# Where a transformer step loads its residual tiles, its first weight and one block's normed rows

## The chip, the cores and the metric

One core of a Trainium2 chip runs the whole program. Its engines are TensorE (PE, matmuls; PEld is its weight load), VectorE (DVE), ScalarE (ACT), GpSimd (POOL) and SyncE (SP), whose queue issues the data transfers here. Each engine takes its instructions strictly in the order in which they are written into its queue, and waits for semaphores on the way. The metric is device time in microseconds for one execution.

## The reference, cut to what matters

One layer of a streaming encoder runs on a prompt of 2048 tokens and a sample of 32, with width 1024, all in float32:

```python
def rmsnorm(x, g, eps=EPS):
    xf = x.astype(jnp.float32)
    y = xf * lax.rsqrt(jnp.mean(xf * xf, axis=-1, keepdims=True) + eps)
    return (y * g.astype(jnp.float32)).astype(x.dtype)

def ffn_ple(h, p, g_mlp, w_up, w_down, w_ple_gate, w_ple_proj):
    c = rmsnorm(h, g_mlp)
    h = h + jnp.square(jax.nn.relu(c @ w_up)) @ w_down
    return h + jax.nn.sigmoid(h @ w_ple_gate) * (p @ w_ple_proj)

# per layer, for the prompt and for the sample:
qa, ka, va, qb, kb, vb = split_proj(rmsnorm(hp, g_attn[i]), w_in[i])
oa = diff_attn_prompt(qa, ka, va, t5_table, lam)
ob = band_attn_prompt(qb, kb, vb, band_table[i])
hp = hp + merge(oa, ob, subln_g[i], out_norm_b[i], w_out[i], lam_init)
hp = ffn_ple(hp, p_prompt[i], g_mlp[i], w_up[i], w_down[i], w_ple_gate[i], w_ple_proj[i])
```

`diff_attn_prompt` and `band_attn_prompt` are two kinds of attention. The change touches neither; it touches the start of the first projection, the MLP and the gate.

## The kernel before, in words

**Precision.** Every float32 operand is split into a high part (`hi`, rounded by ScalarE) and a low part (`lo`, the difference, by VectorE or by GpSimd in pieces of 256 columns). `split` (L232 to 241) does that: L235 is ScalarE's high part, L241 VectorE's low part, L230 and L220 GpSimd's. `mm3` (L257 to 269) then does three matmuls for one product: high by high, low by high, high by low.

**Blocks.** The tokens are cut in four blocks: 0 (512), 1 (512 and the 32 of the sample), 2 and 3 (512 each). `HALVES` is (0, 1) and (2, 3). Activations lie transposed, 128 channels to a tile.

**The front.** `run` loads two tiles of rows of x, the constants, the first unit of the value weights `w_v` (512 KB), and then the first 256 columns of x transposed (`xcols`, two transfers of 512 KB, channels 0 to 511 and 512 to 1023). Three more weight units and the next 256 tokens follow. `prep` takes the squares of the rows (L393), the reciprocal root (`rsqrt`, L275 to 282), spreads it over the partitions with a transpose on TensorE (L397, tile `rp`), scales x with it (L405, tile `xt`) and splits the result into `aH` and `aL`. `proj` makes the value products: for the columns c = 0 and c = 1 of `w_v`, two units each, it splits the weights (`wunit`, tiles `wh` and `wl`), where VectorE does the low parts as long as `spare` is set, as it is in this first call. For the first 256 tokens and c = 0, `mm3` is told `high`: all high by high products come first, then those with the weight's low part, then those with the activation's (L264).

**The MLP of blocks 0 and 1.** `cnorm` fills `cH` and `cL`, the split of the normed rows, tile by tile, eight tiles of 128 channels. For block 1, `cpre` has written the normed rows to the DRAM tensor `cB` while block 0 ran. When block 0's units have been written, `cnorm(1, ...)` loads each row tile into a `tmp` tile and splits it into the one `act` pair, which block 0 has just used. `tmp` has three buffers, and the MLP's own relu tiles (L980, L981) use the same ring. The same pool has the tags `sh` and `sl` (one buffer each) and `acc` (two) of the same size, which the norms use. `mlp_down` adds its products from PSUM into h (L1001); the PSUM pool of these products has two banks here.

**The MLP of blocks 2 and 3.** The two blocks together are computed with seven products in place of eight (a Strassen-like scheme). `uphase` (L1120 to 1194) makes the seven combinations of the activations and stores them in the DRAM tensor `uS`; the stores of the last group stand at the end, after which its tiles' memory is given back. `dphase` (L1196 to 1250) then takes the seven products in the order 3, 5, 7, 4, 2, 6, 1. Each has eight steps c, each step two halves k. For a half it splits the activation (`dx`, four buffers, from `ut`, loaded from `uS`) and the weight (`dw`, from `wd`, or from the combination `dv` of two `wd`), and does 12 matmuls into four PSUM banks (tile `dp`). At a product's end its four banks are added into the tiles of h (L1249): product 3 into block 3's tiles 0 to 7, product 5 into block 2's tiles 0 to 3 and block 3's 0 to 3.

**Where h comes from.** h of blocks 2 and 3 (16 tiles of 256 KB) lies in the DRAM tensor `hS`. Its place in SBUF, `hh`, is where the tiles of `uphase` were. `hstep` is called in product 3 at k = 0 of each step. In the steps 0 to 3 it loads two tiles for each of the two blocks. Ahead of each load stands a copy of one column of the step's `dx` into the tile, on GpSimd (L1698); the load overwrites it, and so it cannot start before that step's `dx` is there, and the `dx` buffer is not free before the copy has read it.

**The gates.** Between the steps of `dphase`, `run` advances `gates()`, the gate of blocks 0 and 1: it loads h of the block in one transfer of 2 MB, splits it (`hH`, `hL`; the low parts of even tiles on GpSimd, of odd ones on VectorE), and then multiplies by `w_ple_gate` (tile `gps`) and `w_ple_proj` (`pps`). The weights, `ut` and `pn` share a ring of four buffers.

**What sets the order.** The program text gives each instruction a priority, and a planner with a simulated clock (`schedule_with_timeline_sim=True`) writes the queues: at each point it takes what it holds to be ready. Buffers and memory that are used again carry semaphore waits. All transfers go through SP's one queue, in order.

Of the kernel before, what the change touches and what calls it, by code (L numbers as in the profile page):

```python
# [12 lines left out]
F32 = mybir.dt.float32  # L13
# [31 lines left out]
HALVES = [(0, 1), (2, 3)]  # L45
# [81 lines left out]
def drain(gen):  # L127
    for _ in gen:
        pass
# [67 lines left out]
class Kern:  # L197
# [175 lines left out]
        self.dma(x[:n], src)  # L373
        return x

    def xcols(self, b, c0, n, pp):
        xt = pp.tile([P, 8, 256], F32, tag="xt", bufs=self.nx, name="xt")
        for k in range(0, 8, 4):
            self.dma(xt[:, k : k + 4, :n], self.xT[:, k : k + 4, T0[b] + c0 : T0[b] + c0 + n])
        return xt  # L380

    def prep(self, b, acts, pp, mm, tag, xs=()):
# [34 lines left out]
    def proj(self, half, grp, acts, sg, mm, vs=range(2), gs=range(4), spare=None):  # L417
        nc, a = self.nc, self.a
# [7 lines left out]
        u = {}  # L426
        for c, b, c0, n in order:
            if c not in u:
                lo = "dve" if spare else "pool"
                u[c] = [  # L430
                    self.wunit(a["w_v"][grp, i, c], [4, 256], "act", lo, spare if (c, i) == (1, 1) else None)
                    for i in range(2)
                ]
            aH, aL = acts[b]
            t0 = 512 * b + c0 if c0 < 512 else SP
            ps = mm.tile([P, 512], F32, tag="mm", name="vps")
            self.mm3(
                ps[:n, :256],
                [
                    (aH[:, k, c0 : c0 + n], aL[:, k, c0 : c0 + n], u[c][k // 4][0][:, k % 4], u[c][k // 4][1][:, k % 4])  # L440
                    for k in range(8)
                ],
                high=bool(spare) and c0 < 256 and c == 0,
            )
            raw = (Rings((spare, "vraw", 4)) if spare else self.vr).tile([P, 256], F32, name="vraw")
            nc.scalar.activation(raw[:n], ps[:n, :256], AF.Copy)
            hl = sg.tile([P, hc, 2, dv], F32R, tag="vhl", bufs=3, name="vhl")
            r3 = raw.rearrange("p (h d) -> p h d", d=dv)
            self.split(hl[:n, :, 0], hl[:n, :, 1], r3[:n], "dve", "pool")
            row = t0 if t0 < SP else t0 + PAST  # L450
            self.dma(
                self.vS[grp][row : row + n, 512 * c : 512 * c + 512],
                hl[:n].rearrange("p a b d -> p (a b d)"),
            )
            if t0 >= SP:
                self.dma(vo_s[0:n, 256 * c : 256 * c + 256], raw[:n])
            elif grp == 0:
                self.dma(vo_p[t0 : t0 + n, 256 * c : 256 * c + 256], raw[:n])
            elif t0 >= SP - 512:
                self.dma(vo_p[t0 - SP + 512 : t0 - SP + 512 + n, 256 * c : 256 * c + 256], raw[:n])  # L460
            yield
# [734 lines left out]
    def dphase(self, h, pool, md, step):  # L1196
        nc = self.nc
        def wrow(q, c):
            i, j = int(q[0]) - 1, int(q[1]) - 1
            r = pool.tile([P, 2, 512], F32, tag="wd", bufs=6, name="wd")  # L1200
            self.dma(r.rearrange("p a b -> p (a b)"), self.a["w_down"][8 * j + c, i])
            return r

        def operands(m, sq, so, c):
            ws = [wrow(q, c) for q in sq]
            u = self.rawp.tile([P, 2, 512], F32, bufs=self.nraw, name="ut")
            self.dma(u, self.uS[:, m - 1, 2 * c : 2 * c + 2])
            for k in range(2):
                x = pool.tile([P, 2, 512], F32R, tag="dx", bufs=4, name="dx")
                self.tsplit(x, u[:, k], "dve")  # L1210
                v = ws[0][:, k]
                if len(ws) == 2:
                    v = pool.tile([P, 512], F32, tag="dv", bufs=4, name="dv")
                    nc.vector.tensor_tensor(v, ws[0][:, k], ws[1][:, k], op=so)
                w = self.wp.tile([P, 2, 512], F32R, tag="wc", bufs=self.wtags[2], name="dw")
                self.tsplit(w, v, "dve")
                yield w, x

        add, sub = ALU.add, ALU.subtract
        plan = [  # L1220
            (3, ("11",), add, (("12", add), ("22", add))),
            (5, ("11", "12"), add, (("11", sub), ("12", add))),
            (7, ("12", "22"), sub, (("11", add),)),
            (4, ("22",), add, (("11", add), ("21", add))),
            (2, ("21", "22"), add, (("21", add), ("22", sub))),
            (6, ("21", "11"), sub, (("22", add),)),
            (1, ("11", "22"), add, (("11", add), ("22", add))),
        ]
        for m, sq, so, outs in plan:
            ps = [md.tile([P, 512], F32, tag="mm", name="dp") for _ in range(4)]  # L1230
            for c in range(8):
                for k, (w, x) in enumerate(operands(m, sq, so, c)):
                    if m == 3 and k == 0:
                        step(c, x)
                    for d in range(4):
                        sl = slice(P * d, P * d + P)
                        self.mm3(
                            ps[d], [(w[:, 0, sl], w[:, 1, sl], x[:, 0], x[:, 1])],
                            start=c + k == 0, stop=c == 7 and k == 1,
                        )  # L1240
                if c < 7:
                    yield
            adds = [(d, q, op) for d in range(4) for q, op in outs]
            if m == 1:
                adds.sort(key=lambda x: x[1])
            for d, q, op in adds:
                i, t = int(q[0]) - 1, int(q[1]) - 1
                hv = h[2 + t][4 * i + d]
                nc.vector.tensor_tensor(hv, hv, ps[d], op=op)  # L1249
            yield  # L1250
# [231 lines left out]
    def run(self):  # L1482
        tc, nc, a = self.tc, self.nc, self.a
        with ExitStack() as top:
# [25 lines left out]
            with ExitStack() as x:  # L1510
                self.nx = 2
                pp = opened(x, "pp0", 3, side="right")
                spare = opened(x, "w4", 1, side="right")
                xs = [self.xrows(0, P * i, P, pp) for i in range(2)]
                self.consts(cp)
                self.pre = [self.wraw(a["w_v"][0, 0, 0], [4, 256])]
                xs.append(self.xcols(0, 0, 256, pp))
                self.pre += [self.wraw(a["w_v"][0, i, c], [4, 256]) for c, i in ((0, 1), (1, 0), (1, 1))]
                xs += [self.xrows(0, 256 + P * i, P, pp) for i in range(2)]
                xs.append(self.xcols(0, 256, 256, pp))  # L1520
                wk = opened(x, "setup", 1, side="right")
                p0 = self.prep(0, acts, pp, ps_t, "tp", xs)
                p1 = self.prep(1, acts, pp, ps_t, "tp")
                su = self.setup(cp, wk, sg)
                for _ in range(5):
                    next(p0)
                front = Rings((mm, "mm"), (ps_s, "s"))
                self.warm(ps_o)
                for i, _ in enumerate(self.proj((0,), 0, acts, sg, front, spare=spare)):
                    if i in (0, 1, 2):  # L1530
                        next(p0, None), next(p0, None)
                    if i in (9, 11, 13, 15):
                        next(su)
                    if i > 7:
                        next(p1, None), next(p1, None)
                drain(su)
                drain(p1)
                self.nx = 1
            ppx = ExitStack()
            pp = opened(ppx, "pp", 1)  # L1540
# [4 lines left out]
            with ExitStack() as x:  # L1545
                pool = opened(x, "a0", 1, side="right")
# [40 lines left out]
            actq = Sized(opened(sq_, "actq", 2), BLK, True)  # L1587
# [9 lines left out]
            wk = opened(sq_, "wk", 1)  # L1597
# [20 lines left out]
            def hmove(b, h, load, ds=range(8)):  # L1618
                for d in ds:
                    x, y = h[d][:, : BN[b]], self.hS[:, d, T0[b] : T0[b] + BN[b]]  # L1620
                    self.dma(*((x, y) if load else (y, x)))
                return h
# [20 lines left out]

            for b in HALVES[0]:
                if b == 1:
                    drain(self.cnorm(1, wk, actq, cn))
                h = [hq.tile([P, BLK], F32, tag="h", bufs=8, name="h") for _ in range(8)]
                hmove(b, h, True)
                dn = Turn(mm)
# [42 lines left out]
            h = {b: hh.tile([P, 8, 512], F32, tag="h", name="h") for b in HALVES[1]}  # L1692
            h = {b: [t[:, d] for d in range(8)] for b, t in h.items()}

            def hstep(c, x):
                for b in HALVES[1] if c < 4 else ():
                    for d in (2 * c, 2 * c + 1):
                        nc.gpsimd.tensor_copy(h[b][d][:, :1], x[:, 0, :1].bitcast(F32))  # L1698
                    hmove(b, h[b], True, range(2 * c, 2 * c + 2))

            fk = opened(top, "fk", 1)
            udx, gqx = ExitStack(), ExitStack()
# [90 lines left out]
```

## Time and profile before

| | |
|---|---|
| median of 3 runs | 2963.94 us (2962.72 to 2965.97) |
| profiled execution | 2962.09 us, of which span 2960.3 us |
| PE busy | 2898.4 us (98%), 17041 matmuls |
| VectorE, ScalarE, GpSimd busy | 1759.7, 1761.3, 1377.7 us |
| data moved | 584.57 MB, mean 197 GB/s |
| mean granted clock of TensorE | 0.993 |

A row of a group or of the order of time names an engine, a line, the operation, and output <- input by the program's tile names; "x8" is a count. In brackets stands how long the engine was idle just before and what ended that wait. A row of the waits reads: who waited for whom, total us, times, longest. A line number can be that of a helper, so tile names say more. Copies and splits of many tiles share a line.

### The profile page before, as it was taken

The numbers are of one execution on the slowest core, as the hardware profiler recorded it, in microseconds if no ns is written. First come the engines' busy times: TensorE is split into PE (matmuls) and PEld (weight loads), VectorE is DVE, ScalarE is ACT, GpSimd is POOL, SyncE is SP. The second block draws the span as 40 slices with busy tenths as digits, with TensorE's granted clock in tenths as the row PEclk, the third lists the DMA queues.
The fourth block names the chain that finished last, engine by engine and source line by source line (L and its number), as shares of the span: only waits on it lengthen the run. The fifth ranks groups of instructions, "written<-read, shape, count | busy, mean of one in ns | idle before, by whom it ended". The sixth has DMA issues, their size and how long they took to land.

```text
span 2960.3 us, 49308 instructions
## 1 busy us (share of the span) xinstructions
PE 2898.4 (98%) x17041; PEld 2556.4 (86%) x17041; DVE 1759.7 (59%) x3930; ACT 1761.3 (59%) x3741; POOL 1377.7 (47%) x1911
## 2 busy tenths in 40 slices
PE   8999999999999999999999999999999989999998
PEld 7898998898889888888899999889788868888886
DVE  6565855444465543665665564447666556767955
ACT  5576757766666665767776675444555445545554
POOL 4677665533345455655554454440855533133000
PEclk9999999999999999999999999999999999999999
DMA  9977578776677644444743433666444395756811
GB/s 352 329 255 235 188 245 268 253 232 198 227 251 229 205 158 155 164 156 151 233 145 120 150 111 114 190 206 204 158 150 145 140 347 186 271 194 200 270 60 57
DMA packets 301513, 584.57 MB, mean 197 GB/s; under 512 B 34864, under 2 KB 132272, under 8 KB 301264
## 3 DMA queue, kind: packets, MB, share of 16 engines
q1 hardware_dynamic: 301264, 581.43, 58.7%
q8 instruction: 135, 2.21, 0.3%
q14 instruction: 114, 0.93, 0.1%
HBM read 450.10 MB, written 131.22 MB: 196 GB/s over the span
## 4 chain that ended last, share of the span: by engine, by line
PE 87%; DMA 5%; DVE 4%; ACT 2%; issue 1%; POOL 1%; SPq 0%; ACTq 0%; DVEq 0%; POOLq 0%
PE s L607 4%; PE ups L269 4%; PE ups L268 4%; PE ups L267 4%; PE qps L267 4%; PE qps L268 4%; PE qps L269 4%; PE dps L267 4%; PE dps L269 4%; PE dps L268 4%; PE xps L269 3%; PE xps L268 3%; PE xps L267 3%; PE dp L267 3%; PE dp L269 3%; PE dp L268 3%
## 5 line engine op out<-in xcount | busy, mean ns | idle before, releaser
L230 POOL TENSOR_TENSOR wl<-wr,wh 128x256 fp32r<-128x256 f32 x936 | 699.0, 778 | 688.9 <-ACT wh L235 600.5
L235 ACT ACTIVATE wh<-wr 128x1024 fp32r<-128x1024 f32 x270 | 284.8, 1056 | 181.5 <-issue 28.7
L267 PE MATMUL dps<-uh,wh 128*128 128x272 f32 (+1 forms) x768 | 249.8, 326 | 5.0 <-DVE h L1001 4.4
L267 PE MATMUL ups<-cH,wh 128*128 128x272 f32 (+1 forms) x768 | 249.1, 325 | 2.0 <-ACT wh L235 1.9
L269 PE MATMUL ups<-cH,wl 128*128 128x272 f32 (+1 forms) x768 | 249.1, 325 | 0.9 <-DVE wl L241 0.9
L268 PE MATMUL ups<-cL,wh 128*128 128x272 f32 (+1 forms) x768 | 249.7, 325 | 0.0
L268 PE MATMUL dps<-ul,wh 128*128 128x272 f32 (+1 forms) x768 | 247.7, 323 | 0.0
L269 PE MATMUL dps<-uh,wl 128*128 128x272 f32 (+1 forms) x768 | 247.4, 323 | 0.0
L267 PE MATMUL qps<-aH,wh 128*128 128x512 f32 (+3 forms) x640 | 229.1, 358 | 2.7 <-ACT wh L235 2.2
L269 PE MATMUL qps<-aH,wl 128*128 128x512 f32 (+3 forms) x640 | 227.5, 356 | 0.0
L268 PE MATMUL qps<-aL,wh 128*128 128x512 f32 (+3 forms) x640 | 227.2, 355 | 0.0
L268 PE MATMUL dp<-dx,dw 128*128 128x512 f32 x448 | 178.0, 397 | 0.0
L267 PE MATMUL dp<-dx,dw 128*128 128x512 f32 x448 | 168.1, 399 | 9.2 <-ACT dx L235 9.1
L607 PE MATMUL s<-ka,q 128*128 128x512 f32 (+3 forms) x640 | 174.2, 369 | 1.3 <-DMA q<-qS 0.7
L269 PE MATMUL dp<-dx,dw 128*128 128x512 f32 x448 | 174.9, 397 | 0.0
L267 PEld LDWEIGHTS dps<-uh,wh 128*128 128x128 f32 x768 | 144.2, 188 | 17.7 <-DVE h L1001 6.1
L267 PEld LDWEIGHTS ups<-cH,wh 128*128 128x128 f32 x768 | 144.4, 188 | 14.9 <-ACT wh L235 2.3
L613 DVE TENSOR_REDUCE nm<-s 128x1 f32<-128x512 f32 (+1 forms) x192 | 121.7, 640 | 57.1 <-PE s L607 55.8
L269 PEld LDWEIGHTS ups<-cH,wl 128*128 128x128 f32 x768 | 144.2, 188 | 12.7 <-DVE wl L241 1.4
L268 PEld LDWEIGHTS ups<-cL,wh 128*128 128x128 f32 x768 | 144.5, 188 | 11.3
L269 PEld LDWEIGHTS dps<-uh,wl 128*128 128x128 f32 x768 | 144.2, 188 | 11.0
L268 PEld LDWEIGHTS dps<-ul,wh 128*128 128x128 f32 x768 | 144.4, 188 | 10.4
(278 smaller groups left out, 8897.1 us busy)
## 6 DMA issues: line engine op xcount, KB each, us to landing
wd<-w_down SPq DMA_DIRECT2D x96, 512.0 KB, 5.1
q<-qS SPq DMA_DIRECT2D x128, 256.0 KB, 4.5
v<-vSa SPq DMA_DIRECT2D x64, 512.0 KB, 3.8
wr<-w_up SPq DMA_DIRECT2D x64, 512.0 KB, 3.7
wr<-w_down SPq DMA_DIRECT2D x64, 512.0 KB, 3.7
wr<-w_qk SPq DMA_DIRECT2D x58, 512.0 KB, 5.0
ut<-uS SPq DMA_DIRECT2D x56, 512.0 KB, 4.1
kS<-qk SPq DMA_DIRECT2D x32, 512.0 KB, 5.1
```

Of the source, the lines that this page charges most:

```text
L230: nc.gpsimd.tensor_tensor(out[:, sl], a[:, sl], b[:, sl], op=op)
L235: nc.scalar.activation(hi, raw, AF.Copy)
L267: nc.tensor.matmul(ps, lh, rh, start=start and i == 0, stop=False)
L268: nc.tensor.matmul(ps, lh, rl, start=False, stop=False)
L269: nc.tensor.matmul(ps, ll, rh, start=False, stop=stop and i == n - 1)
L607: nc.tensor.matmul(s, q[:, m, hl, P * qi : P * qi + nr], kt[:, m, k0 - kb : k0 - kb + n], start=hl == 0, stop=hl == 1)
L613: nc.vector.tensor_reduce(nmx, s, axis=AX.X, op=ALU.max, negate=True)
```

## The change

Three things are edited. In `dphase` the hook `step` is called at k = 0 of every product with its number, and `hstep` now loads one tile per step: block 3's tile c in step c of product 3, block 2's tile c in step c of product 5; the one-column copy ahead of it is on VectorE. In the front, `xcols` may call a function between its two transfers, and the first unit of `w_v` is loaded there, behind the first half of x transposed and not ahead of both; the low parts of the two units of c = 0 move from VectorE to GpSimd. In the MLP, `cnorm` of block 1 takes its row tiles in turn from `tmp`, `sh`, `sl` and `acc` and not from `tmp` alone.

```diff
-    def xcols(self, b, c0, n, pp):
+    def xcols(self, b, c0, n, pp, between=None):
         xt = pp.tile([P, 8, 256], F32, tag="xt", bufs=self.nx, name="xt")
         for k in range(0, 8, 4):
             self.dma(xt[:, k : k + 4, :n], self.xT[:, k : k + 4, T0[b] + c0 : T0[b] + c0 + n])
+            if k == 0 and between:
+                between()
         return xt
...
             if c not in u:
-                lo = "dve" if spare else "pool"
+                lo = "dve" if spare and c else "pool"
...
                 for k, (w, x) in enumerate(operands(m, sq, so, c)):
-                    if m == 3 and k == 0:
-                        step(c, x)
+                    if k == 0:
+                        step(m, c, x)
...
-                self.pre = [self.wraw(a["w_v"][0, 0, 0], [4, 256])]
-                xs.append(self.xcols(0, 0, 256, pp))
+                xs.append(self.xcols(0, 0, 256, pp, lambda: self.pre.append(self.wraw(a["w_v"][0, 0, 0], [4, 256]))))
...
                 if b == 1:
-                    drain(self.cnorm(1, wk, actq, cn))
+                    idle = Rings(*[(wk, t, n) for t, n in (("tmp", 3), ("sh", 1), ("sl", 1), ("acc", 2))])
+                    drain(self.cnorm(1, idle, actq, cn))
...
-            def hstep(c, x):
-                for b in HALVES[1] if c < 4 else ():
-                    for d in (2 * c, 2 * c + 1):
-                        nc.gpsimd.tensor_copy(h[b][d][:, :1], x[:, 0, :1].bitcast(F32))
-                    hmove(b, h[b], True, range(2 * c, 2 * c + 2))
+            def hstep(m, c, x):
+                b = {3: 3, 5: 2}.get(m)
+                if b:
+                    nc.vector.tensor_copy(h[b][c][:, :1], x[:, 0, :1].bitcast(F32))
+                    hmove(b, h[b], True, (c,))
```

`Rings` (L152 to 161) hands out tiles from its rings in turn.

## The prediction

> **What bounds the kernel.** I read the page first, then who TensorE (PE) waited for over the whole span, then the busy time by stretch, and last the instructions in order of time at the three places that the diff touches.
>
> ```profile
> span 2960.3 us, 49308 instructions
> PE 2898.4 (98%) x17041; PEld 2556.4 (86%) x17041; DVE 1759.7 (59%) x3930; ACT 1761.3 (59%) x3741; POOL 1377.7 (47%) x1911
> PE dp L267 <- ACT dx L235: 9.1, 2, 8.4
> PE rp L397 <- DVE rsy L282: 6.0, 1, 6.0
> PE dps L267 <- DVE h L1001: 4.4, 5, 2.0
> PE gps L267 <- ACT wh L235: 3.5, 1, 3.5
> PE qps L267 <- ACT wh L235: 2.2, 1, 2.2
> 0.00:20.00 20.00, 10.49 (x53) 9.88 (x54) 10.77 (x22) 12.86 (x23) 0.93 (x7) 0.74 0.95 336
> 1400.00:1440.00 40.00, 37.61 (x190) 31.36 (x189) 29.22 (x58) 28.47 (x61) 16.44 (x21) 1.00 0.63 201
> 2370.00:2430.00 60.00, 47.73 (x196) 37.38 (x194) 33.77 (x48) 24.54 (x44) 14.36 (x26) 0.94 0.98 378
> ```
>
> TensorE is busy for 2898.4 of 2960.3 us, and no edit takes a matmul away. So the change can only win back part of 61.9 us in which TensorE stands, plus time that it runs at a lower granted clock. In the stretch rows (length, then busy PE, PEld, DVE, ACT, POOL, then clock, DMA share, GB/s) the three places hold 9.5, 2.4 and 12.3 us of it. The first and third are also places where the DMA engines are full (0.95 and 0.98).
>
> **The largest place: the start of the down projection.** These are the instructions in order of time (start, length), the landing times of two loads there, and three stretches of 4 us.
>
> ```profile
> 2393.96 0.69 DVE L241 TENSOR_TENSOR dx<-ut,dx 128x512 fp32r<-128x512 f32 x1 [0.96 <-ACT dx L235]
> 2399.95 0.32 SPq L211 DMA_DIRECT2D uS<-u  x1
> 2400.67 8.74 POOL L220 TENSOR_TENSOR hL<-h,hH 128x256 fp32r<-128x256 f32 x8 [32.48 <-ACT hH L235]
> 2407.62 2.34 DVE L1214 TENSOR_TENSOR dv<-wd 128x512 f32<-128x512 f32 x2
> 2409.36 4.36 POOL L1698 COPY h<-dx 128x1 f32<-128x1 f32 x16
> 2410.39 1.15 ACT L235 ACTIVATE dx<-ut 128x512 fp32r<-128x512 f32 x2 [6.16 <-POOL h L1698]
> 2410.88 11.27 SPq L211 DMA_DIRECT2D h<-hS  x16
> 2411.07 2.07 PE L267 MATMUL dp<-dx,dw 128*128 128x512 f32 x4 [8.40 <-ACT dx L235]
> 2423.20 0.52 SPq L211 DMA_DIRECT2D wr<-w_ple_gate  x1
> 2429.24 1.06 ACT L235 ACTIVATE wh<-wr 128x1024 fp32r<-128x1024 f32 x1 [0.64 <-DMA wr<-w_ple_gate]
> 2430.36 0.50 PE L267 MATMUL gps<-hH,wh 128*128 128x512 f32 x1 [3.51 <-ACT wh L235]
> uS<-u SPq DMA_DIRECT2D x2, 256.0 KB, 5.3
> h<-hS SPq DMA_DIRECT2D x16, 256.0 KB, 5.7
> 2412.00:2416.00 4.00, 4.00 (x14) 3.10 (x13) 2.85 (x5) 2.09 (x5) 1.71 (x4) 0.71 0.99 371
> 2416.00:2420.00 4.00, 4.00 (x19) 3.22 (x18) 0.69 (x1) 0.27 (x1) 0.00 (x0) 1.00 1.05 395
> 2432.00:2436.00 4.00, 4.00 (x13) 3.11 (x13) 4.00 (x4) 2.48 (x4) 4.00 (x5) 0.65 0.73 238
> ```
>
> The chain reads backwards. TensorE waits 8.40 us for a split dx tile. There are four dx buffers, and each even one must first be read by a one-column copy on POOL (L1698). POOL is strictly in order, and its copies stand behind eight low-part pieces of the gate's h, which end at 2409.4. Then SP issues all sixteen loads of h in one burst of 11.27 us, and the gate's weight, queued behind them, lands 6.0 us after 2423.20. That is the second stand of 3.51 us. After each stand the clock is down: 14 and 13 matmuls are counted in 4 us where a full stretch counts 19, one every 0.21 us, so the restarts cost 5 x 0.21 = 1.1 and 6 x 0.21 = 1.3 us. Together 9.1 (both waits for dx) + 3.5 + 2.4 = 15.0 us.
>
> Part by part:
>
> *Copies from POOL to VectorE.* The wait on the eight pieces (2400.67 to 2409.4) goes. What is late next is the memory: h lies where the up phase's tiles lay, and the last of these leaves by the store at 2399.95, which lands 5.3 us later, at 2405.25. The earliest copy is there; ScalarE needs 0.68 us from dx to the matmul (2410.39 to 2411.07), so TensorE resumes at 2406.1 and 5.0 us of the 8.4 are saved. If VectorE, which is in order too, takes the copy only before its dv pair at 2407.62, it resumes at 2408.5 (2.6 saved); behind that pair at 2410.8 (0.3 saved). I take **3.7**, between the two likelier places. The slow restart of 1.1 I leave in.
>
> The Trainium skill ("TensorE: Matmul & The Clock Gate", section "What's actually happening") has the clock fall after an idle window of about 3.4 us; by that rule a stand of 3.4 us or less may restart at full clock, and the sum would be up to 1.1 us better. The row at 2430.36 (3.51 us idle, then 13 matmuls in 4 us) is just on the other side of it, so the trace agrees and leaves it open.
>
> *The loads, one per step.* The sixteen copies need not come in four steps any more: h of block 3 takes the eight steps of the first product, block 2 the eight of the second. At most six of the sixteen loads stand ahead of the gate's weight instead of sixteen; at 11.27 / 16 = 0.70 us each it is issued ten loads, 7.0 us, sooner, at 2416.2, and lands at 2422.2. TensorE gets there at 2426.85 (2430.36 - 3.51) less 3.7, at 2423.1. So the stand goes with its slow restart: **3.5 + 1.3 = 4.8**; if the queue stays as full as it is, nothing.
>
> *What the copies cost.* The trace has no one-column copy on VectorE. Bounds: 0.15 us by the nearest one-column row (L298 below), 0.27 by POOL's 4.36 / 16; sixteen are 2.4 to 4.4 us, hidden because VectorE is 59% busy. Queued behind each are the splits of dw and dx, for which TensorE waits; that is the third rival. The loads must land before the sums of their product: a tile copied with dx of the last step lands 5.7 us after issue, and four dx buffers ahead of the last matmul are four times twelve matmuls at 0.21, 10 us. Covered; without that cover up to 5.7 us.
>
> **The front.** In order of time:
>
> ```profile
> 5.95 0.15 DVE L298 TENSOR_SCALAR columns<-columns 128x1 f32<-128x1 f32 x1 [4.61 <-DMA columns<-columns]
> 7.58 1.06 ACT L235 ACTIVATE wh<-wr 128x1024 fp32r<-128x1024 f32 x1 [0.23 <-DMA wr<-w_v]
> 8.54 0.19 ACT L278 ACTIVATE rsy<-rsy 128x2 f32<-128x2 f32 x1
> 8.67 1.23 DVE L241 TENSOR_TENSOR wl<-wr,wh 128x1024 fp32r<-128x1024 f32 x1 [2.56 <-ACT wh L235]
> 10.70 0.66 PE L397 MATMUL rp<-ident,rsy 128*128 128x128 f32 x2 [6.01 <-DVE rsy L282]
> 11.40 3.22 DVE L405 SCALAR_TENSOR_TENSOR xt<-xt,columns,rp 128x256 f32<-128x256 f32 x8 [0.84 <-PE rp L397]
> 11.83 1.06 ACT L235 ACTIVATE wh<-wr 128x1024 fp32r<-128x1024 f32 x1 [3.10 <-DMA wr<-w_v]
> 13.46 2.07 PE L264 MATMUL vps<-wh,aH 128*128 128x256 f32 x8 [2.10 <-ACT aH L235]
> 33.60 5.67 POOL L230 TENSOR_TENSOR wl<-wr,wh 128x256 fp32r<-128x256 f32 x8 [3.38 <-ACT wh L235]
> 40.66 3.48 DVE L405 SCALAR_TENSOR_TENSOR xt<-xt,columns,rb 128x256 f32<-128x256 f32 x4 [8.55 <-ACT wh L235]
> 46.80 0.50 PE L267 MATMUL qps<-aH,wh 128*128 128x512 f32 x1 [2.20 <-ACT wh L235]
> ```
>
> Today the first weight's high part (1.06) stands ahead of the Exp on ScalarE, and its low part (1.23) ahead of the norm's small ops on VectorE. With the weight a half of x later, the Exp goes first (1.1 sooner) and the low part goes to POOL (1.2 sooner): rp and the first product up to 2.3 us earlier, at 11.2 for 13.46. POOL needs 5.67 / 8 x 4 = 2.8 us for a low part where VectorE needs 1.23; both are wanted only behind the high products, and the second unit's high part cannot begin before its load at 11.83, so its low part ends near 15.7, about when VectorE's did.
>
> POOL's pieces now run beside xt. An xt beside POOL took 3.48 / 4 = 0.87 us at 40.66 (row vector in SBUF), and 3.22 / 8 = 0.40 at 11.40 (row vector in PSUM, POOL idle). At 0.87 the eight xt would end 3.8 us later than at 0.40, and the gain of the second four is gone.
>
> The Trainium skill ("SBUF — State Buffer", section "Who interferes with whom") has a VectorE op with two inputs in SBUF and a reading GpSimd op block each other, which speaks against this edit. Both rows agree with it. At the edited place the vector is in PSUM, so by that rule only the aL splits would slow down and the front's gain would stay whole.
>
> The gain must also pass 46.80, where TensorE waits for a weight that ScalarE takes behind block 1's x, itself not begun before 40.66 with DMA full. If that stays put, all 2.3 us end there, the wait becomes 4.5 and a slow restart (1.3) is new. Bounds: 2.3 saved to 1.3 lost; I take **0.6**, near the middle.
>
> **The block boundary.**
>
> ```profile
> 1422.91 1.33 ACT L235 ACTIVATE cH<-tmp 128x544 fp32r<-128x544 f32 x2 [1.59 <-DMA tmp<-cB]
> 1424.31 0.68 DVE L1001 TENSOR_TENSOR h<-h,dps 128x512 f32<-128x512 f32 x1
> 1425.04 0.50 PE L267 MATMUL dps<-uh,wh 128*128 128x512 f32 x1 [2.03 <-DVE h L1001]
> ```
>
> ScalarE waits for a cB load that had no free tmp buffer, VectorE behind it, and TensorE for VectorE's sum that frees a PSUM bank. With seven buffers for the eight tiles the loads can land before they are wanted. The stretch holds 2.4 us of standing; cH may only be written when block 0 is through with it, so a crowd of splits remains. Bounds 0 to 2.4; I take **1.5**, more than half, as the DMA wait heads the chain.
>
> **Sum:** 3.7 + 4.8 + 0.6 + 1.5 = 10.6 us. The profiled execution took 2962.09 us (span 2960.3 and 1.8 around it), 1.85 under the median 2963.94. So 2951.5 for that one and 2953.3 for the median.
>
> **Rivals.**
>
> A, the forecast, 2953.3, chance 0.45; its own range 2948 to 2957.
>
> B, *the copy stays late*: DMA is full until 2428, the copy falls behind the dv pair, and the small edits bring nothing. 0.3 + 4.8 = 5.1: 2958.8, chance 0.2. For it: the share of 0.98. Against: ten loads less in the queue.
>
> C, *VectorE takes over POOL's wait*, the slower side. If the first copy stands ahead of the split at 2393.96, VectorE stands from there to 2405.25. TensorE, which stopped at 2402.67 (2411.07 - 8.40), then misses the last two tiles (2 x 12 x 0.21 = 5.0 us), runs dry at 2397.7 and waits 8.3 to 2406.0, the copy and a split of 0.69 later. VectorE's queue from the row at 2393.96 to that at 2407.62, thirteen ops, is 12.5 us of work, with the splits for the next products partly behind the gate's: 1.3 and 7.7 us more of standing (estimates from those lengths). With three slow restarts of 1.2 and no wait for the gate that is 20.9 against 15.0 today: 2963.94 + 5.9 = 2970. It decides once VectorE stands longer than about 7 us. Against it: before, the order put the copies after the gate's pieces, so the planner does know them to be late. Chance 0.15.
>
> D, *all three places clear*: 15.0 + 2.4 + 2.3 = 19.7: 2944.2, chance 0.1. Against: the store lands at 2405.25.
>
> E, *it does not do what it says*: the planner places all instructions anew, the loads still bunch since the copies wait for the same memory, and the stands only move: 2964, chance 0.1.
>
> **How the numbers follow.** This kernel's runs differ by 0.1%, so I count 0.2% (5.9 us, below 2958.0 or above 2969.9) as a difference. Faster: nearly all of A, D, and 0.07 of B: 0.6. Slower: half of C and some of what a new order may upset elsewhere: 0.13. The same: 0.27. The range runs from D's end, 2944, over A, B and E to 2966, and leaves out C and half of D.
>
> **What would show it.** First stand: TensorE's wait for dx in the new trace is 3 to 6 us in place of 8.4, and no gps wait follows; sixteen VectorE copies lie apart by some 5 us each. Front: the first vps product before 12.5 us, and the wait before qps near 45 grown or not. Boundary: cH splits without DMA waits. I am wrong if VectorE's longest wait before a copy exceeds 7 us, if a wait for the h sums appears at the end of the first product, or if the wait for dx keeps its length.

## The result and the profile after

The changed kernel takes 2973.61 us (median of 6 runs, 2972.48 to 2976.2) against 2963.33 for the kernel before in the same session: a ratio of 1.0038 with a 95% interval of 1.0028 to 1.0048. It is 10.3 us slower. 2953.3 was forecast, with a range up to 2966. In the experiments below four single runs, at a granted clock of 0.75 to 0.85, took 190 to 575 us longer than their kernel's others; the ratios leave them out, and without them the medians given here would move by at most 0.8 us.

The page's head of the changed kernel:

```profile
span 2971.1 us, 49299 instructions
PE 2907.4 (98%) x17041; PEld 2563.0 (86%) x17041; DVE 1761.7 (59%) x3944; ACT 1760.1 (59%) x3741; POOL 1386.8 (47%) x1903
```

Its list of what TensorE waited for (total us, times, longest):

```profile
PE dp L267 <- ACT dx L235: 8.8, 2, 8.1
PE rp L399 <- DVE rsy L282: 3.9, 1, 3.9
PE dps L267 <- DVE h L1003: 2.9, 4, 0.9
```

Its busy time in two stretches (length, busy PE, PEld, DVE, ACT, POOL with counts, granted clock, DMA share, GB/s):

```profile
0.00:60.00 60.00, 48.53 (x284) 42.95 (x285) 37.24 (x80) 35.93 (x75) 29.74 (x42) 0.91 1.01 359
720.00:780.00 60.00, 51.41 (x264) 42.15 (x264) 36.93 (x146) 42.90 (x100) 8.36 (x14) 0.86 0.64 198
```

The same two stretches of the kernel before:

```profile
0.00:60.00 60.00, 48.29 (x294) 43.80 (x295) 36.00 (x85) 37.28 (x78) 24.32 (x37) 0.91 1.01 361
720.00:780.00 60.00, 58.90 (x316) 49.49 (x315) 30.45 (x110) 36.88 (x80) 14.56 (x21) 1.00 0.63 210
```

The list of waits reads as hoped: the wait for `rp` is 2.1 us shorter, that for the gate's weight (`gps`, 3.5 before) is gone, and the whole standing time (span less PE busy) is 63.7 us for 61.9. What grew is PE's busy time, by 9.0 us for the same 17041 matmuls, while the mean granted clock went from 0.993 to 0.991. Both lead to a place that no edit touches: from 720 to 780 us TensorE stands 8.6 us in place of 1.1, in pieces of at most 1.7 us, and the clock is 0.86. There the second half of the projection and the band attention run side by side.

The place of the down projection, in order of time, changed kernel:

```profile
2416.64 0.32 SPq L211 DMA_DIRECT2D uS<-u  x1
2424.05 2.34 DVE L1216 TENSOR_TENSOR dv<-wd 128x512 f32<-128x512 f32 x2
2426.31 0.32 DVE L1700 COPY h<-dx 128x1 f32<-128x1 f32 x4
2426.48 2.19 ACT L235 ACTIVATE dx<-ut 128x512 fp32r<-128x512 f32 x4 [5.83 <-DVE h L1700]
2427.16 2.07 PE L267 MATMUL dp<-dx,dw 128*128 128x512 f32 x4 [8.07 <-ACT dx L235]
```

TensorE resumes here 16.1 us later than before (2411.07), but the span ends only 10.8 us later. So some 16 us were lost ahead of this place and 5 won behind it. The copies stand behind the `dv` pair, and the wait for `dx` is 0.3 us shorter, no more.

### The profile page after: what moved, and what is told of

It reads as the page before. It is cut to its first block, busy times and chain, and to the rows that moved or that the text cites. A ratio compares the mean times of both kernels' runs of the same rounds, so it can differ in the third digit from the quotient of the medians.

```text
span 2971.1 us, 49299 instructions
## 1 busy us (share of the span) xinstructions
PE 2907.4 (98%) x17041; PEld 2563.0 (86%) x17041; DVE 1761.7 (59%) x3944; ACT 1760.1 (59%) x3741; POOL 1386.8 (47%) x1903
## 4 chain that ended last, share of the span: by engine, by line
PE 64%; DVE 2%; DMA 2%; ACT 1%; issue 0%; POOL 0%; SPq 0%; ACTq 0%; DVEq 0%; POOLq 0%
PE ups L269 4%; PE ups L268 4%; PE ups L267 4%; PE dps L267 4%; PE dps L269 4%; PE dps L268 4%; PE dp L267 4%; PE dp L268 4%; PE dp L269 4%; PE xps L269 3%; PE xps L268 3%; PE xps L267 3%; PE s L609 3%; PE gps L269 2%; PE gps L268 2%; PE gps L267 2%
## 5 line engine op out<-in xcount | busy, mean ns | idle before, releaser
L230 POOL TENSOR_TENSOR wl<-wr,wh 128x256 fp32r<-128x256 f32 x944 | 708.3, 781 | 707.7 <-ACT wh L235 615.0
L267 PE MATMUL dps<-uh,wh 128*128 128x272 f32 (+1 forms) x768 | 249.6, 326 | 3.3 <-DVE h L1003 2.9
L267 PE MATMUL ups<-cH,wh 128*128 128x272 f32 (+1 forms) x768 | 249.2, 325 | 1.9 <-ACT wh L235 1.9
L267 PE MATMUL qps<-aH,wh 128*128 128x512 f32 (+3 forms) x640 | 227.5, 355 | 3.1 <-ACT wh L235 1.4
L267 PE MATMUL dp<-dx,dw 128*128 128x512 f32 x448 | 167.9, 399 | 8.8 <-ACT dx L235 8.8
L790 DVE CUSTOM_DVE_ANT_0 eb<-sb,bb 128x320 f32<-128x320 f32 (+2 forms) x232 | 104.2, 478 | 93.6 <-PE tpb L802 85.4
L267 PEld LDWEIGHTS dps<-uh,wh 128*128 128x128 f32 x768 | 144.3, 188 | 15.2 <-DVE h L1003 4.0
L267 PEld LDWEIGHTS ups<-cH,wh 128*128 128x128 f32 x768 | 144.5, 188 | 14.5 <-ACT wh L235 2.3
L622 ACT ACTIVATE e<-s,nm 128x512 f32<-128x512 f32 (+1 forms) x192 | 124.1, 651 | 51.8 <-DVE nm L615 32.4
```

Source lines behind the costliest of these rows:

```text
L230: nc.gpsimd.tensor_tensor(out[:, sl], a[:, sl], b[:, sl], op=op)
L267: nc.tensor.matmul(ps, lh, rh, start=start and i == 0, stop=False)
L622: nc.scalar.activation(dst, src, AF.Exp, bias=nmx, scale=1.0 if near is None else -1.0, accum_out=z[:nr, m, bi : bi + 1],)
L790: nc.vector.tensor_tensor_reduce(e[:, w * i : w * i + w], s, bb[:nr, b0 + w * i : b0 + w * i + w], 1.0, -3e38, ALU.add, ALU.max, st[:, 3 + ...
```

## The experiments

All medians stand beside that of the kernel before in the same session (2962.88, 2963.05 and 2962.43 us in the order of the three groups); the ratio has its 95% interval.

### Each edit alone

The front's two edits without the others; the edit of h; the edit of the rows; and the last two together.

> The kernel before with the two edits of the front alone (first weight between the halves of x transposed; low parts of the units of c = 0 on GpSimd). Theory 1 (the front's edits make the planner write another order for the band attention's second half, near 720 to 780 us, where TensorE then runs without the query projection as filler and its clock falls): slower than before by 13 to 20 us, about 2979, with the clock near 0.8 to 0.9 in 720 to 780 as in the changed kernel, and a first product near 11.0 us. Theory 2 (the loss belongs to the other edits, which reach back through the planner): within 2 us of before, clock 1.00 in 720 to 780. Theory 3 (the front's own order costs at the front): slower, but the distance is there by 60 us.

> The kernel before with the edit of the loads of h alone (copies on VectorE, one tile per step). Theory 1: everything up to 2370 us as before, the wait of TensorE for dx near 2405 stays at about 8 us since the copies come behind the dv pair, and the wait for the gate's weight with its slow restart goes: faster by 3.5 to 6 us, about 2958.5. Theory 2: slower than before. If VectorE's wait for the first copy held up the splits: slower by 5 to 10 us.

> The kernel before with the edit of block 1's normed rows alone (row tiles from four rings). Theory 1: everything up to the units of block 0 as before, ScalarE's waits for the row loads near 1420 to 1440 gone, TensorE stands up to 2.4 us less there: faster by 0 to 2.5 us, about 2962. Theory 2 (the four rings take tiles that the norms beside it want): slower by some us, with new waits near 1400 to 1450.

> The edits of the loads of h and of the normed rows together, the front as before. Theory 1: the two gains add, faster than before by 4 to 8 us, about 2957, and faster than the changed kernel by 15 to 19 us. Theory 2: as slow as the changed kernel, or near it.

| edit | us | ratio |
|---|---|---|
| front | 2978.38 | 1.0049 (1.0036 to 1.0062) |
| loads of h | 2958.74 | 0.9983 (0.9973 to 0.9993) |
| rows of block 1 | 2962.14 | 0.9997 (0.9988 to 1.0006) |
| loads of h and rows | 2957.15 | 0.9982 (0.9973 to 0.9991) |

The front costs 15.5 us, the other two together win 5.7, and the sum, 9.8, is what the changed kernel lost (10.3). The distance is not there at 60 us: in the front's run 286 matmuls are counted up to then, for 294 before, and eight at 0.16 us each are 1.3 us. One part of the expectation was off: in the front's profiled execution the clock is 1.00 up to 760 us and only 0.91 in the next 20. The stands are there all the same.

### What happens at 720 us

Busy time of L267 alone (the first of the three matmuls of a projection term) in one stretch, first of the kernel before, then of the changed one:

```profile
730.00:770.00 40.00, 14.33 (x36) 6.76 (x36) 1.00 0.76 251
```

```profile
730.00:770.00 40.00, 0.00 (x0) 0.00 (x0) 0.82 0.65 203
```

In order of time, the loads of the norm's raw rows and the first `css` product of block 1 in the kernel before, and then, in the changed kernel, the `css` products of block 0, a store of the attention, the loads of the raw rows, the square that waits for them, and the `css` products of block 1:

```profile
742.50 2.29 SPq L211 DMA_DIRECT2D oraw<-oT  x3
748.57 0.39 PE L952 MATMUL css<-sh,ones_r 128*128 128x272 f32 x1 [0.58 <-ACT sh L235]
```

```profile
717.99 0.39 PE L954 MATMUL css<-sh,ones_r 128*128 128x512 f32 x1
718.22 0.40 PE L955 MATMUL css<-sl,ones_r 128*128 128x512 f32 x1
757.69 0.56 SPq L211 DMA_DIRECT2D oT<-t  x1
761.44 1.75 SPq L211 DMA_DIRECT2D oraw<-oT  x4
764.27 0.66 ACT L851 ACTIVATE oraw<-oraw 128x544 f32<-128x544 f32 x1 [2.10 <-DMA oraw<-oT]
767.71 0.52 PE L954 MATMUL css<-sh,ones_r 128*128 128x272 f32 x2 [0.34 <-ACT sh L235]
```

In the program the norm of the attention's outputs (`onorm`, L840) is woven into the last projection: `weave2` with `ONP = (16, 1, 6)` puts the `css` of block 1 after 24 units, with eight units of `qps` behind it. These `css` need the rows of block 1, which the band attention of the first two pairs of tiles stores, and they take one of the two PSUM banks (`mm`) that the projection uses in turn. In the kernel before, the loads of these rows were issued from 742.50 on, the `css` of block 1 came at 748.57, and the projection never stopped. In the changed kernel the loads follow a store at 757.69 and the `css` comes at 767.71, while the projection had done its 24 units before 730. It stands until 772, and for over 40 us the attention runs alone. Its matmuls wait for each other's softmax (from 715 to 775 us 3.6 us for `stb`, 1.7 for `pHb`, 1.7 for `pLb`), so TensorE stands between them.

What that costs follows from the rows: from 720 to 780 us there are 18 and not 57 matmuls of L267, so 3 x 39 = 117 fewer of 512 columns. In order of time such matmuls start 0.23 us apart where TensorE does not stand, so that is 27 us; against it stand 65 more matmuls, most of them the attention's of 128 to 320 columns (4 to 10 us at the same rate). By this estimate the changed kernel is 17 to 23 us behind.

The gap stands in the kernel's instruction order: in the row of TensorE's matmuls, 40576 columns of attention follow each other with no projection among them. In the order before, the longest such row from 600 to 900 us has 5504 columns. So the planner wrote it.

### Which edit of the front, and how much a gap costs

```diff
-                lo = "dve" if spare else "pool"
+                lo = "dve" if spare and c else "pool"
```

```diff
+            if k == 0 and between:
+                between()
```

> The kernel before with only the low parts of the units of c = 0 on GpSimd. In the order of its matmuls the norm's products (css) stand where they stood before, with no gap in the projection behind them. Theory 1 (the loss comes from that gap): within 2 us of before, 2961 to 2965, and the front's gain of some tenths, if any, is lost in it. Rival (GpSimd's slow low parts cost the loss): slower by more than 5 us.

> The kernel before with only the first weight's load between the two halves of x transposed. In the order of its matmuls 19584 columns of attention stand in one row with no projection among them, behind the last css but one; with both edits of the front it is 40576 columns, and those cost 15.5 us. Theory 1 (the gap costs by its length): slower by about 15.5 x 19584 / 40576 = 7.5 us, 2968 to 2973. Rival (the load itself costs, or the low parts do): as slow as both edits together, 2978, or no slower than before.

The low parts on GpSimd alone: 2966.29 us, 1.0007 (0.9997 to 1.0017), a little above the range that was expected (2961 to 2965) and not to be told from before. The moved load alone: 2970.49, 1.0026 (1.0017 to 1.0035), 7.4 us slower where 7.5 was worked out from the length of its gap.

Then a gap was made in the kernel before, without any of the edits:

```diff
-ONP = (16, 1, 6)
+ONP = (16, 1, 1)
```

> The kernel before, none of the three edits, with the norm's two css products five projection units earlier in the program (ONP (16, 1, 1) for (16, 1, 6)). In the order of its matmuls 28288 columns of attention then stand without projection. Theory 1 (the gap costs by its length, whatever makes it): slower by 15.5 x 28288 / 40576 = 10.8 us, 2971 to 2977, with a stretch of low clock or many short stands near 720 to 770. Rival (the gap is harmless, and the loss comes with the front's edits): within 2 us of before.

2972.66 us, 1.0033 (1.0021 to 1.0045): 10.2 us slower for 10.8 expected. The stretch, in which TensorE stood 1.1 us before, now reads

```profile
700.00:740.00 40.00, 33.42 (x188) 26.80 (x187) 25.51 (x103) 30.30 (x70) 5.87 (x9) 0.92 0.67 223
740.00:780.00 40.00, 40.00 (x209) 34.12 (x210) 18.10 (x64) 22.14 (x48) 11.03 (x16) 1.00 0.58 185
```

The kernels with gaps of 19584, 28288 and 40576 columns are 7.4, 10.2 and 15.5 us slower than the kernel before: about 0.37 us per 1000 columns, whichever line made the gap. The intervals of the three would also allow 0.2 to 0.5.

These are differences of whole kernels, and their orders differ outside the gap too. The traces give an estimate for the gap alone: count the work by matmuls, each at its usual spacing in the kernel before (0.233 us for 512 columns, 0.147 for 320, 0.119 for 256), and compare the times at which two kernels have done the same work. Across its gap the kernel with the moved load falls 9.6 us behind the kernel before, that with the earlier `css` 15.6, that with both edits of the front 18.8 and the changed kernel 22.9. That is 0.46 to 0.56 us per 1000 columns. The last two were some 4 us ahead when their gap began: the projection that they lacked in it had been used up earlier.

### Closing the gap

With all three edits kept, the `css` were put later (first diff), and in another kernel the four steps of the bias setup in the front one projection unit earlier (second diff).

```diff
-ONP = (16, 1, 6)
+ONP = (16, 1, 14)
```

```diff
-                    if i in (9, 11, 13, 15):
+                    if i in (8, 10, 12, 14):
```

> The changed kernel, with the two css products of the norm eight projection units later in the program (ONP (16, 1, 14) for (16, 1, 6)); nothing else differs. In the order of its matmuls the gap shrinks from 40576 to 17728 columns. Theory 1 (the projection stops since the css of block 1 wait for the first half's attention and hold a PSUM bank ahead of it): 8 to 10 us faster than the changed kernel, 2963 to 2966. Rival (the loss comes from elsewhere in the new order): as slow as the changed kernel, 2973.

> The changed kernel, with the four steps of the bias setup in the front one projection unit earlier (8, 10, 12, 14 for 9, 11, 13, 15); all three edits are in. In the order of its matmuls the norm's products stand where they stood before the change, and no gap is left. Theory 1 (of the changed kernel's loss all comes from the gap in the order, nothing from the moved load or from GpSimd's low parts as such): clock 1.00 and no stand above 1.5 us in 720 to 780, and the gains of the other edits come through: 2955 to 2959, 14 to 18 us faster than the changed kernel. Rival (the front's edits cost by themselves): 2965 to 2973.

The first missed: 2977.84 us, 1.0045 (1.0031 to 1.006), no faster than the changed kernel. Where it was aimed it did what it should: L267 runs through,

```profile
730.00:770.00 40.00, 15.88 (x40) 7.54 (x40) 1.00 0.55 183
```

and TensorE stands later and for a shorter time, from 780 to 800 us, in the gap of 17728 columns that is left. By the count of work above this gap loses 9.9 us, some 13 less than the changed kernel's (0.56 us per 1000 columns). But the order behind it is another one too, and a new loss lies from 1810 us on, where the last attention runs out. Busy time by stretch of this kernel:

```profile
780.00:800.00 20.00, 16.48 (x79) 13.62 (x80) 13.52 (x48) 15.04 (x35) 3.09 (x6) 0.91 0.77 255
1810.00:1820.00 10.00, 7.74 (x40) 5.98 (x39) 8.02 (x17) 8.51 (x23) 3.90 (x5) 0.83 0.18 61
1840.00:1880.00 40.00, 34.24 (x214) 29.35 (x213) 18.00 (x25) 20.02 (x39) 14.29 (x20) 1.00 0.46 149
1880.00:1890.00 10.00, 10.00 (x38) 7.99 (x37) 3.09 (x4) 3.34 (x6) 6.41 (x8) 0.84 0.77 249
```

From 1790 to 1920 TensorE is busy 121.98 of 130 us; in the kernel before 127.23, with 849 matmuls there and 777 here. By the same count this kernel falls 10 us further behind from 1810 to 1890 us, and some 4 us near 1430, so what the shorter gap saved went elsewhere. Its median alone does not show what the gap costs.

The second closes the gap altogether: in its instruction order the `css` stand where they stood before the change. It takes 2958.92 us, 0.9987 (0.9977 to 0.9996), 14.7 faster than the changed kernel by the medians of two sessions, whose medians of the kernel before lie 0.9 us apart. Of the changed kernel's three edits none is missing; the stretch is as before the change:

```profile
720.00:780.00 60.00, 58.26 (x311) 49.00 (x310) 30.48 (x110) 36.95 (x81) 14.69 (x22) 1.00 0.63 210
```

So the loss belongs to the order, not to the load or the low parts as such. Against the two other edits alone (2957.15, 0.9982) the front's edits with the gap closed bring nothing that can be measured.

### The loads of h: engine or spreading

One tile per step, copies left on GpSimd:

```diff
-                    nc.vector.tensor_copy(h[b][c][:, :1], x[:, 0, :1].bitcast(F32))
+                    nc.gpsimd.tensor_copy(h[b][c][:, :1], x[:, 0, :1].bitcast(F32))
```

> The kernel before, with h loaded one tile per step (block 3 in product 3, block 2 in product 5) but the one-column copies left on GpSimd. Theory 1 (of the edit of h only the spreading pays; the copy's engine saved 0.3 us): the wait for dx stays at 8.4 us, the wait for the gate's weight goes, 2958 to 2960. Rival (VectorE's copies are what brought it): no faster than before.

2957.40 us, 0.9981 (0.9972 to 0.9990), the same as with VectorE's copies (2958.74, 0.9983). The wait for `dx` is 8.04 us, that for `gps` gone. The spreading is the gain; VectorE's part is nothing that the runs show. (2958 to 2960 were expected.)

Then the copies on ScalarE (`nc.scalar.activation(..., AF.Copy)`), first with the old front, then with the changed kernel whose setup steps stand one unit earlier:

> The edits of the loads of h and of the normed rows, the front as before, and the one-column copies on ScalarE in place of VectorE. On ScalarE they stand right behind the gate's eight high parts (hH), ahead of the dx splits that wait for them. Theory 1 (the first stand lasts since the copies come behind VectorE's dv pair, and h's memory is free some 4 us sooner): TensorE's wait for dx shrinks from 8.1 to about 4 us, 2952 to 2954. Rival (the memory of h, or DMA, holds the copies): the wait stays at 8 us, 2957.

> As the run with the setup steps one unit earlier, and the one-column copies on ScalarE. Theory 1: TensorE's wait for dx 5.2 us in place of 8.1, 2952 to 2957, the fastest so far. Rival: no faster than with the copies on VectorE.

2956.11 us, 0.9975 (0.9966 to 0.9985), and 2955.81 us, 0.9977 (0.9967 to 0.9988). These are the fastest two of all kernels here, 0.6% under the changed kernel and 0.2% under the one before; their intervals overlap those with VectorE's copies, so against these no gain is shown (2952 to 2954 had been expected of the first). The rows, in order of time, of the first:

```profile
2404.07 0.48 ACT L1699 ACTIVATE h<-dx 128x1 f32<-128x1 f32 x4 [2.54 <-DMA uS<-c]
2404.46 2.17 ACT L235 ACTIVATE dx<-ut 128x512 fp32r<-128x512 f32 x4
2405.13 2.07 PE L267 MATMUL dp<-dx,dw 128*128 128x512 f32 x4 [5.15 <-ACT dx L235]
```

The wait for `dx` shrinks to 5.15 us (about 4 were expected; 4.92 in the second of the two kernels), and now the copy waits for the last stores of `uS`: this is the memory that the prediction named. That it sets the floor of this place unless those stores leave sooner is an argument; no run moves them.

## Why the prediction was wrong, step by step

**The step that failed** is the front's price, "bounds 2.3 saved to 1.3 lost", and with it case E, "the planner places all instructions anew ... and the stands only move: 2964, chance 0.1". I priced the edit only from 0 to 60 us, where its rows are. The planner indeed wrote another order, but the stands did not only move: at 720 us an existing dependency (`css` of block 1 behind the first half's attention) turned from met just in time into 40 us without projection, 15.5 us. The chance of a slower kernel, 0.13, did allow for "what a new order may upset elsewhere", but no rival gave that a place, a price or a sign of being wrong. The slower side that I did price, VectorE in POOL's wait (C), did not occur: VectorE's copies started at 2426.31 with no wait of its own ahead of them.

Without the front's edits the forecast would still have been too high: 10.6 us were forecast and 0.6 of them for the front, and the two other edits win 5.7 by the medians. That is rival B, "the copy stays late", 0.3 + 4.8 = 5.1. One of the prediction's own signs of being wrong came true as well: the wait for `dx` keeps its length, 8.07 us for 8.40.

**The front itself** went as worked out at its first step: the first product at 11.02 us (11.2 forecast, 13.46 before).

```profile
8.61 0.66 PE L399 MATMUL rp<-ident,rsy 128*128 128x128 f32 x2 [3.92 <-DVE rsy L282]
11.02 2.07 PE L264 MATMUL vps<-wh,aH 128*128 128x256 f32 x8 [1.75 <-ACT aH L235]
29.77 0.39 PE L269 MATMUL vps<-wh,aL 128*128 128x256 f32 x1 [1.35 <-DVE aL L241]
42.13 0.50 PE L267 MATMUL qps<-aH,wh 128*128 128x512 f32 x1 [1.42 <-ACT wh L235]
```

The 2.4 us were given back by 60 us, to the wait at 29.77 and others (from 25 to 30 us 28 matmuls are counted for 44 before): up to 60 us it is 284 for 294, at 0.16 us each (48.29 / 294) 1.6 us behind. The wait before `qps` did not grow (1.42 for 2.20). For the front by itself the 0.6 was too hopeful, and the loss lies a little past the bad end of its bounds (1.3 lost).

**The port.** VectorE's groups of the first 120 us (busy us, mean ns, idle before), of the kernel before and then of the changed one:

```profile
L241 DVE TENSOR_TENSOR aL<-xt,aH 128x512 fp32r<-128x512 f32 (+1 forms) x20 | 11.2, 588 | 0.0
L405 DVE SCALAR_TENSOR_TENSOR xt<-xt,columns,rp 128x256 f32<-128x256 f32 x16 | 6.4, 475 | 1.9 <-PE rp L397 1.9
```

```profile
L407 DVE SCALAR_TENSOR_TENSOR xt<-xt,columns,rp 128x256 f32<-128x256 f32 x16 | 6.4, 477 | 1.7 <-PE rp L399 0.8 <-DMA ckn<-cb_k 0.8
L241 DVE TENSOR_TENSOR aL<-xt,aH 128x512 fp32r<-128x512 f32 (+1 forms) x20 | 14.3, 755 | 0.0
```

`aL`, with both inputs in SBUF, went from 588 to 755 ns (748 with the low parts moved alone, 606 with the load moved alone); `xt` with its row vector in PSUM stayed at 475 to 477. By the rule of the Trainium skill ("SBUF — State Buffer", section "Who interferes with whom") just these two should behave so; the trace agrees, and the 0.87 us per `xt` that I feared did not come. The means hide the size. In order of time, in the changed kernel:

```profile
9.31 3.23 DVE L407 SCALAR_TENSOR_TENSOR xt<-xt,columns,rp 128x256 f32<-128x256 f32 x8 [0.84 <-PE rp L399]
10.53 8.36 POOL L230 TENSOR_TENSOR wl<-wr,wh 128x256 fp32r<-128x256 f32 x8 [9.05 <-ACT wh L235]
12.44 4.18 DVE L241 TENSOR_TENSOR aL<-xt,aH 128x512 fp32r<-128x512 f32 x4
```

The `xt` take 0.40 us each, as before with GpSimd idle (3.22 for eight), though GpSimd's pieces begin among them. The four `aL` beside those pieces take 1.05 each, where a single one alone takes 0.69. GpSimd's pieces suffer too: 1.05 each, where 5.67 / 8 = 0.71 was counted on, so the two low parts end at 18.89 and not near 15.7.

**The copies, 3.7 forecast, 0.3 found.** Of the three places that I named for the copy, the last came true, behind the `dv` pair. I took a middle value where one of three places had to come out, each with its own price. An early place exists, on ScalarE: 5.15 us of wait for 8.40, though not the 5.0 saved of the earliest copy that I had worked out.

**The loads one per step, 4.8 forecast.** Right in mechanism and size: the gate's wait (3.51) and its slow restart are gone, and the edit alone wins 4.1 us by the medians. From the end of the wait for `dx` to the end of the span its trace takes 2958.4 - 2413.82 us, 4.7 less than before (2960.3 - 2411.07); with GpSimd's copies it is 5.0 less (2949.8 - 2405.61). The copies do not lie 5 us apart at first; four go at once.

**The boundary, 1.5 forecast.** The mechanism shows, ScalarE waits once for a row load and not four times:

```profile
1430.37 1.74 ACT L235 ACTIVATE cH<-tmp 128x544 fp32r<-128x544 f32 x3
1439.01 0.66 ACT L235 ACTIVATE cH<-tmp 128x544 fp32r<-128x544 f32 x1 [1.17 <-DMA tmp<-cB]
1440.17 0.64 ACT L235 ACTIVATE cH<-tmp 128x544 fp32r<-128x544 f32 x1
```

The splits end at 1440.8 after 10.4 us, where they took 21.6 before. Its worth is 0.7 us by the medians, and the interval holds both nothing and 1.5, so the size is not shown.

**A small error of reading.** "One every 0.21 us" comes from counting 19 matmuls in 4 us, and the count takes in those that only reach into the stretch; in order of time they start 0.23 us apart. The two slow restarts become 1.2 and 1.4 us for 1.1 and 1.3, which changes nothing else.

**Open** is why the planner, told of one load in another place, lets the projection run ahead of the attention by 725 us. The runs show only that it does, that the four setup steps one unit earlier undo it, and that a longer gap costs more, about in proportion.

## What to carry to other kernels

Where a planner writes the queues, an edit at the front is priced with the whole order: compare the order of the matmuls before and after, and look for stretches in which the latency-bound work has lost its filler. A dependency that is met just in time (here the norm's product, in the ring of PSUM banks that the filler uses) is the place to look at first, and a bystander's position, a setup step one unit earlier, can bring the old order back. Test each edit alone before any is believed: two of the three edits here were worth 5.7 us and lay hidden under a loss of 15.5 by the third.

## What the runs showed of the hardware

A low clock without a long stand. In the changed kernel the clock falls to half at 730 us, though none of TensorE's waits from 725 to 745 lasts longer than 1.36 us, and it stays there for 10 us in which TensorE is almost fully busy, by slow matmuls:

```profile
730.00:735.00 5.00, 3.05 (x15) 2.37 (x13) 3.17 (x13) 4.61 (x11) 3.52 (x6) 0.65 0.53 169
735.00:740.00 5.00, 5.00 (x25) 4.79 (x23) 2.23 (x10) 3.41 (x9) 0.00 (x0) 0.50 0.75 251
740.00:745.00 5.00, 4.85 (x18) 3.83 (x19) 3.16 (x16) 3.18 (x11) 0.00 (x0) 0.50 0.71 234
```

With the front's edits alone and the same gap, the profiled execution has 1.00 in these three rows; it is the fastest of five, which go from 2971.57 to 2981.55 us, with mean clocks of 0.995 and 0.991. So the clock in such a stretch differs between executions of one order; that this makes the whole spread of the five is not shown, since the four others have no trace. The Trainium skill ("TensorE: Matmul & The Clock Gate", section "What's actually happening") lets the clock fall after an idle window of about 3.4 us; no stand of that length is in these rows. Here the clock fell among three short ones, 0.59, 1.36 and 0.59 us within 5 us; in the front's trace three of 0.59, 0.81 and 0.59 us at the same place left it at 1.00. What decides between the two is open.
